# The output projection of a decoder layer as seven products of half matrices for eight, with the merge before it by pairs of column tiles and the mixer's first products in another order

## The chip, the core and the metric

One core of a Trainium2 chip runs the whole layer in one launch. Its engines are TensorE (PE in the rows; PEld is its loading of weights), VectorE (DVE), ScalarE (ACT), GpSimd (POOL) and SyncE (SP), which here only issues transfers. Each engine takes its instructions strictly in order and waits on semaphores for the others. The metric is device time in microseconds (us).

## The reference

```python
def reference(x, norm_mix, w_in, ...):
    ...
    gate_a, gate_b = jnp.split(jax.nn.sigmoid(g_merge), 2, axis=-1)
    merged = gate_a * (o_a @ w_up_nsa[layer]) + gate_b * (o_b @ w_up_gla[layer])
    x = x + merged @ w_out[layer]
    h = rmsnorm(x, norm_ffn[layer])
    x = x + (jax.nn.silu(h @ w_ffn_gate[layer]) * (h @ w_ffn_up[layer])) @ w_ffn_down[layer]
    return rmsnorm(x, norm_final)
```

`x` is 1024 tokens by 1024 channels, float32. Ahead of this stand two token mixers, `o_a` (sparse attention) and `o_b` (gated linear attention). `w_out` is 1024 by 1024, the SwiGLU's hidden width is 2816.

## The kernel before

All activations lie transposed: 128 channels on the partitions, tokens along the row. A tile of output is 128 channels by 512 tokens; `m` counts the eight tiles of channels (`NM`), `hf` the two halves of the tokens, `MH` is 4. A product of two float32 matrices is taken as three products of rounded parts: each operand is split into a high part (ACT copies it into the rounded type) and a low part (the operand less its high part, on POOL for weights, on DVE for activations), and PE does high x high, high x low and low x high. So each 128-channel block of the sum costs three matmuls of 128x512.

The stages that matter here, in the program's order:

- **Merge** (`merge_job`, L1324). For `m` = 0 to 7 and both halves PE multiplies the mixers' outputs with `w_up`; ACT takes the sigmoid of the gates `zz`, DVE and POOL gate and add. `let_merged` (L1317) then splits the result into the high and low part of a tile `mg`, 16 tiles in all. The product with `o_b` was computed earlier for the five `m` of `UP`; the other three do it here, with twice the PE work.
- **Output projection** (`out_job`, L1373). For each half, then each `m`, PE sums the eight blocks `mg` times `w_out` in one bank: 24 matmuls. DVE adds the bank to the tile `xn` of `x` (L1379), ACT squares it (L1383) and stores it to DRAM, DVE adds the squares up in `sacc` (L1388). The weights come through three rotating pairs of buffers: ACT makes `wh` (L368), POOL makes `wl` (L369).
- **Root.** When a half is complete, `two_parts` splits `sacc` into `sqh` and `sql`, `total` (L1409) lets PE sum them over the partitions with two matmuls (L1412), and `rms_root` (L447) makes `rbc` with two ACT and four DVE instructions. In the projection's second half DVE, ACT and DVE make the normalised first half (`first_block`, L1422): scale (L1426), high part, low part (L1429). `pairs[0].early` (L1460) splits the first four weights of the mixer ahead of time.
- **Channel mixer.** `Pair` holds one pair of weight tiles of the gate or of the up projection. The first three pairs use eight products of half matrices (`EIGHT`), the other nineteen seven (`SEVEN`). A half-matrix product (`Pair.product`, L1476) has 12 matmuls. `todo` is the list of products, in the program's order.

PE's order is the order in which the program is written, and so is DVE's through the mixer's first 26 products. ACT, POOL and SP are ordered by the scheduler of the framework, except where `keep_in_program_order` pins an instruction.

Of the kernel before, what the change touches and what calls it, by code (L numbers as in the profile page):

```python
# [10 lines left out]
F32 = mybir.dt.float32  # L11
# [91 lines left out]
SCRATCH = 2048  # L103
FINE, NGATE, AHEAD = 3, 2, 1200

UP = (1, 2, 4, 5, 7)


class Plan:
# [130 lines left out]
def layer_kernel(ctx, tc, a, outT):  # L240
# [1083 lines left out]
    def merge_job(m):  # L1324
        def make(getw):
            out, ps = [], {}
            for hf in range(2):
                def keep_ps(p, hf=hf):
                    ps[hf] = p

                def evac(p, hf=hf):
                    zz, u = fetched.pop((m, hf))
                    za, zb = zz[:, 0, :], zz[:, 1, :]
                    fetch()
                    tc.keep_in_program_order(S.activation(zz, zz, AF.Sigmoid))
                    let_merged(m - (hf == 0))
# [22 lines left out]
    mcst.release()  # L1359

# [3 lines left out]
    sacc = [None, None]  # L1364
    XN = {}

    last = []

    def let_last():
        while last:  # L1370
            last.pop(0)()

    def out_job(hf, m):  # L1373
        def make(getw):
            def evac(p):
                xv = XN[hf, m] = mid("xn")
                sq = mid("sacc")
                SP.dma_start(xv, a["xT"][:, m, hs(hf)])
                V.tensor_add(xv, p, xv)  # L1379

                def squares():

                    tc.keep_in_program_order(S.activation(sq, xv, AF.Square))  # L1383
                    S.dma_start(x1d[hf][m], xv)
                    if m == 0:
                        sacc[hf] = sq
                    else:
                        V.tensor_add(sacc[hf], sacc[hf], sq)  # L1388

                last.append(squares)  # L1390
                if m == NM - 1:
                    let_last()
            out = products(getw, ps_m, [t[:, 0, :] for t in mg[hf]], [t[:, 1, :] for t in mg[hf]], 0, evac)
            out[5:5] = [(0.0, let_last)]
            return out
        return a["w_out"][m], make
# [5 lines left out]
    def two_parts(t):  # L1402

        h, l = mid("sqh", F32R), mid("sql", F32R)
        tc.keep_in_program_order(S.activation(h, t, AF.Copy))
        tc.keep_in_program_order(P.tensor_tensor(l, t, f(h), OP.subtract))
        return h, l

    def total(st, parts, r):  # L1409

        for i, t in enumerate(parts):
            PE.matmul(st, onesr, t, start=i == 0, stop=i == 1)  # L1412
        rms_root(st, 512, float(D), r, [mid("nv"), mid("nq")])

    XB = {}

# [170 lines left out]
    fill.add(placed(dense([out_job(0, m) for m in range(NM)], False),  # L1587
                    [(15 + 6 * n, 0.0, lambda fn=fn: load(None, None, fn)) for n, fn in enumerate(first_loads())] + [(37 + 11 * n, 0.0, lambda nm=nm: pairs[0].early(nm)) for n, nm in enumerate(("11", "12", "21", "22"))]))
    fill.flush()
    work = dense([out_job(1, m) for m in range(NM)], False)  # L1590
    half_sums = {}
    fill.add(placed(work, [(11, 0.0, lambda: half_sums.update({0: two_parts(sacc[0])})),
                           (15, 450.0, lambda: total(ps_o(), half_sums[0], rbc[:, hs(0)]))]
                    + [(26 + 6 * m, 0.0, lambda m=m: first_block(m)) for m in range(NM)]))
    fill.flush()
    rows.release()


# [27 lines left out]


    MAKE = [[] for _ in range(26)]
    for n in range(NM):

        MAKE[1 + 3 * n // 4] += [(lambda n: normed(1, n), n)] + [(second_block, n - 1)] * (n > 0)
    MAKE[7].append((second_block, NM - 1))
# [17 lines left out]
    for i, (q, s) in enumerate(todo):  # L1650
        if i == 0:

            order.enter_context(tc.manual_schedule(engines={mybir.EngineType.DVE}))
        if i == 26:
            order.close()
        q.product(*s)
        if not q.kept and ahead:
            prepare(ahead.popleft())
        if i == 0:
            half_sums[1] = two_parts(sacc[1])  # L1660
        if i == 1:
            total(ps_o(), half_sums[1], rbc[:, hs(1)])
# [279 lines left out]
```

## Time and profile before

| | |
|---|---|
| median of three runs | 1577.27 us (1574.28, 1577.27, 1579.19) |
| the profiled execution | 1573.65 us |
| its span, first to last instruction | 1571.8 us |
| PE busy | 1556.8 us (99%) |
| DVE, ACT, POOL busy | 1014.1, 810.0, 719.7 us |

The page gives shares of the whole span; the stages have different limits. The merge ends and the projection begins at 831.5 us, the mixer's first matmul starts at 919.1 us. How to read the rows: `out<-in` are the program's names, `x` after them is how many instructions a row stands for, and in brackets stands the idle time before an instruction and what ended it.

### The profile page before, as it was taken

How to read it: one execution, taken by the hardware profiler on the slowest of the kernel's cores; microseconds unless marked ns; L12 is line 12 of the kernel's file. 1: busy time of each engine (PE TensorE's matmuls, PEld its weight loads, DVE VectorE, ACT ScalarE, POOL GpSimd, SP SyncE). 2: the span in 40 equal slices, each digit the busy share in tenths (PEclk: the TensorE clock that was granted, in tenths of full speed). 3: DMA queues.
4: the chain of work that ended last, by engine and by line, in shares of the span. 5: the costliest groups of instructions: out<-in, count | busy, mean ns of one | idle time of the engine just before them, and what ended most of it. 6: DMA issues, size and time to landing. Idle time of an engine off the chain costs nothing.

```text
span 1571.8 us, 23022 instructions
## 1 busy us (share of the span) xinstructions
PE 1556.8 (99%) x8031; PEld 1310.1 (83%) x8031; DVE 1014.1 (65%) x1630; ACT 810.0 (52%) x1615; POOL 719.7 (46%) x635
## 2 busy tenths in 40 slices
PE   9999999999999999999999999999999999999998
PEld 7888988888888888888888888888888888888887
DVE  7780487686777687667574577644444444499785
ACT  6241555575676686677654454334433334454542
POOL 6110466563223353253256520666666666555570
PEclk9999999999999999999999999999999999999999
DMA  5431112232111221131656622323222222795422
GB/s 180 140 104 62 61 55 79 97 107 81 45 51 57 71 83 56 51 109 60 205 184 211 215 83 81 114 101 106 102 101 101 101 101 101 282 340 161 141 88 107
DMA packets 109656, 179.86 MB, mean 114 GB/s; under 512 B 13394, under 2 KB 30435, under 8 KB 109540
## 3 DMA queue, kind: packets, MB, share of 16 engines
q1 hardware_dynamic: 105508, 171.96, 32.5%
q10 hardware_dynamic: 4032, 6.44, 1.1%
q8 instruction: 63, 1.03, 0.3%
q14 instruction: 53, 0.43, 0.1%
HBM read 128.27 MB, written 45.88 MB: 111 GB/s over the span
## 4 chain that ended last, share of the span: by engine, by line
PE 93%; DVE 4%; ACT 1%; issue 1%; DMA 1%; POOL 0%; SPq 0%; DVEq 0%; ACTq 0%; POOLq 0%
PE m L427 19%; PE d L427 10%; PE m L1484 9%; PE m L1485 9%; PE m L1483 9%; PE m L1873 4%; PE m L1871 4%; PE m L1872 4%; PE o L1210 4%; PE t L1201 3%; PE s L1122 2%; PE s L1123 2%; PE t L745 2%; PE t L747 1%; PE t L746 1%; PE t L880 1%
## 5 line engine op out<-in xcount | busy, mean ns | idle before, releaser
L369 POOL TENSOR_TENSOR wl<-wf,wh 128x512 fp32r<-128x512 f32 x106 | 146.3, 1385 | 275.6 <-ACT wh L368 274.8
L1484 PE MATMUL m<-xt,wh 128*128 128x512 f32 x412 | 160.3, 389 | 0.0
L1483 PE MATMUL m<-xt,wh 128*128 128x512 f32 x412 | 160.3, 389 | 0.0
L1485 PE MATMUL m<-xt,wl 128*128 128x512 f32 x412 | 160.3, 389 | 0.0
L1400 POOL TENSOR_TENSOR wl<-ws,wh 128x512 fp32r<-128x512 f32 x76 | 107.5, 1419 | 73.6 <-ACT wh L1399 73.6
L1400 POOL TENSOR_TENSOR wl<-wr,wh 128x512 fp32r<-128x512 f32 x69 | 92.0, 1333 | 70.0 <-ACT wh L1399 70.0
L1179 DVE TENSOR_TENSOR ptl<-t,pth 128x512 fp32r<-128x512 f32 (+1 forms) x168 | 99.5, 596 | 34.4 <-ACT pth L1178 31.4
L1399 ACT ACTIVATE wh<-wr 128x512 fp32r<-128x512 f32 x87 | 55.0, 632 | 121.0 <-POOL wl L1400 90.4
L1399 ACT ACTIVATE wh<-ws 128x512 fp32r<-128x512 f32 x76 | 48.0, 632 | 131.7 <-PE m L1484 112.6
L1178 ACT ACTIVATE pth<-t 128x512 fp32r<-128x512 f32 (+1 forms) x168 | 87.8, 524 | 53.2 <-PE t L1201 45.5
L1871 PE MATMUL m<-xb,wh 128*128 128x512 f32 x280 | 109.1, 389 | 0.3 <-DVE g L1545 0.3
L1400 POOL TENSOR_TENSOR wl<-wd,wh 128x512 fp32r<-128x512 f32 x56 | 82.1, 1468 | 58.9 <-ACT wh L1399 58.7
L1872 PE MATMUL m<-xb,wh 128*128 128x512 f32 x280 | 109.0, 389 | 0.0
L1873 PE MATMUL m<-xb,wl 128*128 128x512 f32 x280 | 108.9, 389 | 0.0
L1400 DVE TENSOR_TENSOR xb<-ar,xb 128x512 fp32r<-128x512 f32 x73 | 82.5, 1150 | 28.8 <-ACT xb L1399 28.8
L368 ACT ACTIVATE wh<-wf 128x512 fp32r<-128x512 f32 x106 | 66.2, 627 | 67.5 <-PE m L427 19.7
L427 PE MATMUL m<-hh,wh 128*128 128x512 f32 x240 | 99.9, 416 | 0.0
L427 PE MATMUL m<-hh,wl 128*128 128x512 f32 x240 | 93.8, 391 | 0.0
L427 PE MATMUL m<-hl,wh 128*128 128x512 f32 x240 | 93.6, 390 | 0.0
L1483 PEld LDWEIGHTS m<-xt,wh 128*128 128x128 f32 x412 | 77.4, 188 | 16.2
L1484 PEld LDWEIGHTS m<-xt,wh 128*128 128x128 f32 x412 | 77.4, 188 | 16.0
L1485 PEld LDWEIGHTS m<-xt,wl 128*128 128x128 f32 x412 | 77.4, 188 | 16.0
(422 smaller groups left out, 4569.4 us busy)
## 6 DMA issues: line engine op xcount, KB each, us to landing
ar<-actd SPq DMA_DIRECT2D x77, 256.0 KB, 3.0
wf<-in_w_t SPq DMA_DIRECT2D x58, 256.0 KB, 2.7
wr<-in_w_gate SPq DMA_DIRECT2D x44, 256.0 KB, 2.7
wr<-in_w_upf SPq DMA_DIRECT2D x44, 256.0 KB, 2.6
wd<-in_w_down SPq DMA_DIRECT2D x33, 256.0 KB, 5.1
zd<-zt SPq DMA_DIRECT2D x32, 256.0 KB, 2.0
zz<-zd SPq DMA_DIRECT2D x16, 512.0 KB, 4.6
wf<-in_w_out SPq DMA_DIRECT2D x32, 256.0 KB, 3.3
```

Source lines behind the costliest of these rows:

```text
L369: P.tensor_tensor(tl, wf, f(th), OP.subtract)
L427: PE.matmul(st["p"], w, x, start=k + i == 0, stop=k == n - 1 and i == 2)
L1178: S.activation(th[:, :c], pt[:, :c], AF.Copy)
L1179: V.tensor_tensor(tl[:, :c], pt[:, :c], f(th[:, :c]), OP.subtract)
L1399: S.activation(th, src, AF.Copy)
L1400: eng.tensor_tensor(tl, src, f(th), OP.subtract)
L1483: PE.matmul(ps, wh[:, c], xh, start=first and k == 0, stop=False, skip_group_check=not first)
L1484: PE.matmul(ps, wh[:, c], xl, start=False, stop=False, skip_group_check=not first)
L1485: PE.matmul(ps, wl[:, c], xh, start=False, stop=k == MH - 1, skip_group_check=not first)
L1871: PE.matmul(dst, wh[:, c], xh, start=first and p == 0, stop=False, skip_group_check=not first)
L1872: PE.matmul(dst, wh[:, c], xl, start=False, stop=False, skip_group_check=not first)
L1873: PE.matmul(dst, wl[:, c], xh, start=False, stop=p == NP - 1, skip_group_check=not first)
```

## The change

The 1024x1024 product is cut into halves in all three directions (channels in, channels out, tokens). Before, that is eight products of half matrices; now it is seven, after Winograd's form. They need sums of half matrices: of the weights S1 to S4 (`s1_out` to `s4_out`) and of the activations T1 to T4 (`t1_out` to `t4_out`). `OUT7` lists the products with the bank each adds to, and the order. One of its entries takes four steps, one for each tile `mp` of output channels, so there are 28 steps of 12 matmuls each. A bank is kept over several products, and after each step DVE adds it to an `xn` tile (`add_out`, L1691), so there are 28 such adds for 16 before.

The merge now goes by pairs of column tiles (`MO`: 0, 4, 1, 5, 2, 6, 3, 7), and `UP` holds 6 for 5. `let_merged` makes, of the second half's tiles 0 to 3, no `mg` but the difference to the first half (`xy`, T1), and POOL takes it from the tile `m + 4` (T2).

While a step runs, an order written out by hand (`todo_out`, `front_out`) places the work of DVE, POOL and ACT on the stretch: those three engines are now under `manual_schedule`. Weights are split by `prep_out`, three steps ahead (wh on ACT, wl on POOL). The squares' sums of the second half go to POOL, but two. The mixer's first eight products use the activations of block 11 first, in both pairs (`todo`); `high_part` and `low_part` make these from the end of the projection on, and `NEXT` places the second half's root after the mixer's first products.

```diff
-UP = (1, 2, 4, 5, 7)
+UP = (1, 2, 4, 6, 7)
...
+    MO = [m for j in range(MH) for m in (j, j + MH)]
+    halves = deque((m, hf) for m in MO for hf in range(2))
...
+    def let_merged():
+        if not merged:
+            return
+        za, hf, m = merged.pop()
+        j = m % MH
+        if hf and m < MH:
+            t = XY[j] = row("xy", shape=(2, 512))
+            V.tensor_sub(t[:, 0, :], za, firsts.pop(j))
+            return
+        t = mg[hf][m] = row("mg", F32R, (2, 512))
+        tc.keep_in_program_order(S.activation(t[:, 0, :], za, AF.Copy))
+        V.tensor_tensor(t[:, 1, :], za, f(t[:, 0, :]), OP.subtract)
+        if m < MH:
+            firsts[j] = za
+        elif hf:
+            x, y = XY[j][:, 0, :], XY[j][:, 1, :]
+            P.tensor_tensor(y, za, x, OP.subtract)
...
-    fill.add(dense([merge_job(m) for m in range(NM)], ready=early))
+    fill.add(dense([merge_job(m) for m in MO], ready=early))
...
+    first_out = [half_weights(a["w_out"][m], 0) for m in range(3)]
...
-    todo = [(q, s) for n in (0, 4) for q in pairs[:2] for s in EIGHT[n:n + 4]]
+    todo = [(q, EIGHT[n]) for ns in ((0, 2), (1, 3)) for q in pairs[:2] for n in ns]
+    todo += [(q, s) for q in pairs[:2] for s in EIGHT[4:]]
...
+    def s3_out(mp):
+        t = OW["S3", mp] = OW["11", mp]
+        V.tensor_sub(t, t, OW["21", mp])
+
+    def s2_out(mp):
+        t = OW["S2", mp] = OW["x", mp][:, 1, :]
+        P.tensor_tensor(t, OW["22", mp], OW["S3", mp], OP.subtract)
...
+    OUT7 = [("11", "11", "A", True, (0, 0)), ("12", "21", "B", True, (0, 0)), ("S2", "T2", "A", False, (1, 0)),
+            ("S3", "T3", "A", False, (1, MH)), ("22", "T4", "A", False, (0, MH)), ("S1", "T1", "B", True, (1, MH)),
+            ("S4", "22", "B", False, (1, 0))]
+    steps = [(p, mp) for p in OUT7 for mp in range(MH)]
...
+    def t3_out(j):
+        t = tmp["T3", j] = mid("to")
+        V.tensor_sub(t, XY[j][:, 1, :], f(mg[0][j][:, 0, :]))
+        V.tensor_sub(t, t, f(mg[0][j][:, 1, :]))
...
+    def place_out(nm, j):
+        parts_of(tmp.pop((nm, j)), OX[nm, j])
...
+    def pinned(src, th, tl, eng):
+        tc.keep_in_program_order(S.activation(th, src, AF.Copy))
+        tc.keep_in_program_order(eng.tensor_tensor(tl, src, f(th), OP.subtract))
+
+    def prep_out(i):
+        (nm, *_), mp = steps[i]
+        wh = wpool.tile([128, 512], F32R, name="wh", bufs=3)
+        wl = wpool.tile([128, 512], F32R, name="wl", bufs=3)
+        pinned(OW[nm, mp], wh, wl, P)
...
+    def add_out(i):
+        (_, _, bank, _, to), mp = steps[i]
+        xv = XN[to[0], to[1] + mp]
+        V.tensor_add(xv, PSB[bank, mp], xv)
...
+        at_out(5 + mp, t3_out, mp)
+        at_out(6 + mp, place_out, "T3", mp)
+        at_out(9 + mp, t4_out, mp)
+        at_out(10 + mp, place_out, "T4", mp)
+        at_out(14 + mp, t1_out, mp)
...
+        at_out(14 + mp, s1_out, mp)
+        at_out(14 + mp, s4_out, mp)
+        at_out(14 + mp, square_of, 0, mp)
+        at_out(15 + mp, square_sum, 0, mp)
...
+    front_out = {20: [lambda: square_of(0, NM - 1), lambda: square_sum(0, NM - 1), lambda: two_parts(0)]}
+    at_out(21, total, 0)
+    at_out(22, total_root, 0)
...
+    with tc.manual_schedule(engines={mybir.EngineType.DVE, mybir.EngineType.Pool, mybir.EngineType.Activation}):
+        for i in range(len(steps)):
+            product_out(i)
+            if i:
+                add_out(i - 1)
+            for fn in front_out.get(i, ()):
+                fn()
+            if i + 3 < len(steps):
+                prep_out(i + 3)
+            for fn in todo_out[i]:
+                fn()
...
-            q.prep(s, V if 3 <= i < 26 else P)
+            q.prep(s, V if 14 <= i < 26 else P)
...
+    NEXT = {0: [lambda: low_part(0, 5), lambda: high_part(0, 6), lambda: square_sum(1, MH - 1)],
+            1: [lambda: two_parts(1), lambda: low_part(0, 6), lambda: high_part(0, 7)],
+            2: [lambda: low_part(0, 7), lambda: total(1)], 3: [lambda: total_root(1)]}
```

What this does to the order of instructions, at three places. First DVE at the start of the projection's stretch in the kernel before. `minus` and `minusr` are two constants for the last stage, `xn<-m,xn` is the add of a bank to `x`, `sacc` the sum of squares:

```order
L1778 CAST minusr<-minus 128x128
L1379 TENSOR_TENSOR xn<-m,xn 128x512 x2
L1388 TENSOR_TENSOR sacc<-sacc 128x512
L1379 TENSOR_TENSOR xn<-m,xn 128x512
L1388 TENSOR_TENSOR sacc<-sacc 128x512
```

One add and one sum of squares stand there for each 24 matmuls of PE. Now DVE in the changed kernel, at steps 6 to 8 (L1645, L1646: the two subtractions that make a T3 in `to`; L1667: the low part of a T3, written over `mg`; L1691: the add):

```order
L1691 TENSOR_TENSOR xn<-m,xn 128x512
L1667 TENSOR_TENSOR mg<-to,mg 128x512
L1645 TENSOR_TENSOR to<-xy,mg 128x512
L1646 TENSOR_TENSOR to<-to,mg 128x512
L1691 TENSOR_TENSOR xn<-m,xn 128x512
```

Between two adds, that is per step of 12 matmuls, three instructions now stand on DVE that read two tiles of SBUF each. Next the end of the first half on DVE in the changed kernel (steps 18 to 22; `sql` is the low part of the sum of squares, `nv` and `rbc` the root):

```order
L1691 TENSOR_TENSOR xn<-m,xn 128x512
L1396 TENSOR_TENSOR sacc<-sacc 128x512 x2
L1691 TENSOR_TENSOR xn<-m,xn 128x512
L1396 TENSOR_TENSOR sacc<-sacc 128x512
L1404 TENSOR_TENSOR sql<-sacc,sqh 128x512
L1691 TENSOR_TENSOR xn<-m,xn 128x512 x2
L451 TENSOR_SCALAR nv<-o 128x512
```

The low part `sql` comes after all the sums, and it was POOL's before (L1406). Last PE around the two matmuls that add up the first half's squares, before and then now:

```order
L427 MATMUL m<-mg,wl 128x512
L1412 MATMUL o<-sqh,onesr 128x512
L1412 MATMUL o<-sql,onesr 128x512
L427 MATMUL m<-mg,wh 128x512 x2
L427 MATMUL m<-mg,wl 128x512
```

```order
L1684 MATMUL m<-xb,wh 128x512
L1685 MATMUL m<-xb,wh 128x512
L1686 MATMUL m<-xb,wl 128x512
L1410 MATMUL o<-sqh,onesr 128x512
L1410 MATMUL o<-sql,onesr 128x512
L1684 MATMUL m<-xb,wh 128x512
```

Before, they stood in the third product of the second half, with 13 products still to come before the mixer. Now they stand behind step 21 of 0 to 27, six steps before the mixer. PE has 48 matmuls fewer in all (7832 for 7880).

## Rows read from the trace of the kernel before

**Rows 1.** Page, part 1 (busy us) and part 4 (the chain's engines).
```profile
PE 1556.8 (99%) x8031; PEld 1310.1 (83%) x8031; DVE 1014.1 (65%) x1630; ACT 810.0 (52%) x1615; POOL 719.7 (46%) x635
...
PE 93%; DVE 4%; ACT 1%; issue 1%; DMA 1%; POOL 0%; SPq 0%; DVEq 0%; ACTq 0%; POOLq 0%
```

**Rows 2.** Stretches: us, then busy us of PE PEld DVE ACT POOL, clock.
```profile
781.00:831.50 50.50, 50.50 (x224) 41.84 (x223) 39.11 (x47) 27.49 (x38) 28.15 (x20) 1.00 0.52 167
831.50:918.80 87.30, 87.30 (x386) 72.27 (x385) 51.00 (x57) 38.16 (x65) 49.32 (x36) 1.00 0.65 211
918.80:982.00 63.20, 63.20 (x280) 52.27 (x280) 48.18 (x72) 30.77 (x50) 4.72 (x3) 1.00 0.19 67
```

**Rows 3.** Timeline of PE: first matmuls of the projection, first of the mixer.
```profile
831.51 0.62 PE L427 MATMUL m<-mg,wh 128*128 128x512 f32 x2
...
919.08 0.39 PE L1483 MATMUL m<-xb,w 128*128 128x512 f32 x1
```

**Rows 4.** Groups of PE by line and shape: count, busy us, mean ns.
```profile
L427 PE MATMUL m<-mg,wh 128*128 128x512 f32 x256 | 78.9, 389 | 0.0
...
L427 PE MATMUL m<-mg,wl 128*128 128x512 f32 x128 | 49.8, 389 | 0.0
```

**Rows 5.** Waits of PE from 600 to 1300 us: total, times, longest.
```profile
PE t L1201 <- DVE ptl L1179: 1.0, 2, 0.7
```

**Rows 6.** Groups of DVE, 831.5 to 945 us.
```profile
L1388 DVE TENSOR_TENSOR sacc<-sacc 128x512 f32<-128x512 f32 x14 | 15.8, 1127 | 11.7 <-ACT sacc L1383 11.5
L1379 DVE TENSOR_TENSOR xn<-m,xn 128x512 f32<-128x512 f32 x16 | 11.0, 686 | 20.2 <-DMA xn<-in_xT 19.5 <-PE m L427 0.7
...
L1419 DVE SCALAR_TENSOR_TENSOR xn<-xn,gains,rbc 128x512 f32<-128x512 f32 x8 | 5.9, 748 | 0.0
...
L1429 DVE TENSOR_TENSOR xb<-xn,xb 128x512 fp32r<-128x512 f32 x8 | 5.5, 688 | 1.7 <-ACT xb L1428 1.4
```

**Rows 7.** Timeline of DVE: start us, us, instruction.
```profile
838.14 1.21 DVE L1778 CAST minusr<-minus 128x128 fp32r<-128x128 f32 x1
...
885.48 1.67 DVE L454 TENSOR_TENSOR nv<-nv,nq 128x512 f32<-128x512 f32 x1
...
888.94 0.68 DVE L1379 TENSOR_TENSOR xn<-m,xn 128x512 f32<-128x512 f32 x1
889.54 0.73 DVE L1426 SCALAR_TENSOR_TENSOR xn<-xn,gains,rbc 128x512 f32<-128x512 f32 x1
...
892.01 1.36 DVE L1388 TENSOR_TENSOR sacc<-sacc 128x512 f32<-128x512 f32 x1 [0.35 <-ACT sacc L1383]
```

**Rows 8.** Timeline of POOL, the same stretch and the merge's end.
```profile
835.03 4.25 POOL L369 TENSOR_TENSOR wl<-wf,wh 128x512 fp32r<-128x512 f32 x3 [3.29 <-ACT wh L368]
...
885.19 1.41 POOL L369 TENSOR_TENSOR wl<-wf,wh 128x512 fp32r<-128x512 f32 x1 [2.70 <-ACT wh L368]
...
891.54 2.99 POOL L369 TENSOR_TENSOR wl<-wf,wh 128x512 fp32r<-128x512 f32 x2 [3.07 <-ACT wh L368]
```

**Rows 9.** Groups of POOL and of ACT, 831.5 to 945 us.
```profile
L369 POOL TENSOR_TENSOR wl<-wf,wh 128x512 fp32r<-128x512 f32 x30 | 42.9, 1442 | 35.0 <-ACT wh L368 34.9
L1464 POOL TENSOR_TENSOR w<-wr,w 128x512 fp32r<-128x512 f32 x4 | 5.2, 1292 | 0.0
...
L368 ACT ACTIVATE wh<-wf 128x512 fp32r<-128x512 f32 x30 | 18.7, 625 | 25.3 <-DVE xn L1379 11.7 <-PE m L427 6.6 <-DMA wf<-in_w_out 3.2
L1383 ACT ACTIVATE sacc<-xn 128x512 f32<-128x512 f32 x16 | 9.9, 620 | 4.8 <-DVE xn L1379 4.8
...
L450 ACT ACTIVATE nq<-o,eps 128x512 f32<-128x512 f32 x2 | 1.4, 688 | 5.3 <-PE o L1412 3.2 <-DVE xn L1379 2.1
```

**Rows 10.** Page, part 6: issues, KB each, us to landing.
```profile
wf<-in_w_out SPq DMA_DIRECT2D x32, 256.0 KB, 3.3
```

More of the change, by code (lines that the diff above doesn't have):

```diff
@@ L1365, in layer_kernel @@
     XN = {}
[L1367 to L1396, printed above, removed]
     def split(src, th, tl, eng):
@@ L1400, in split, with square_of, square_sum, two_parts @@
         eng.tensor_tensor(tl, src, f(th), OP.subtract)
[L1402 to L1411, printed above, removed]
+    def square_of(hf, m):
+        t = SQ[hf, m] = mid("sacc")
+        S.activation(t, XN[hf, m], AF.Square)
+        S.dma_start(x1d[hf][m], XN[hf, m])
+    def square_sum(hf, m):
+        t = SQ.pop((hf, m))
+        if sacc[hf] is None:
+            sacc[hf] = t
+        else:
+            (P if hf and m not in (MH - 2, MH - 1) else V).tensor_tensor(sacc[hf], sacc[hf], t, OP.add)
+    SQ, half_sums, root_tmp = {}, {}, {}
+    def two_parts(hf):
+        h, l = half_sums[hf] = mid("sqh", F32R), mid("sql", F32R)
+        S.activation(h, sacc[hf], AF.Copy)
+        V.tensor_tensor(l, sacc[hf], f(h), OP.subtract)
+    def total(hf):
+        st = root_tmp[hf] = ps_o()
+        for i, t in enumerate(half_sums[hf]):
             PE.matmul(st, onesr, t, start=i == 0, stop=i == 1)
-        rms_root(st, 512, float(D), r, [mid("nv"), mid("nq")])
+    def total_root(hf):
+        rms_root(root_tmp[hf], 512, float(D), rbc[:, hs(hf)], [mid("nv"), mid("nq")])
     XB = {}
@@ L1585, in placed @@
         return work
[L1587 to L1594, printed above, removed]
@@ L1595, in layer_kernel, with load_out @@
-    fill.flush()
+    OW, PSB = {}, {}
+    def load_out(nm, mp):
+        if nm == "21":
+            OW["x", mp] = fa.tile([128, 2, 512], F32, name="wx", tag="xT3", bufs=MH)
+            t = OW["x", mp][:, 0, :]
+        else:
+            tag, bufs = ("ws", 4) if nm == "11" or ("S3", mp) in OW else ("w7", 6)
+            t = fa.tile([128, 512], F32, name="wo", tag=tag, bufs=bufs)
+        OW[nm, mp] = t
+        m, o = mp + MH * (nm[0] == "2"), MH * (nm[1] == "2")
+        load(t, a["w_out"][m][:, o:o + MH, :].rearrange("p a b -> p (a b)"))
@@ new lines, in layer_kernel, with parts_of, t2_out @@
+    steps = [(p, mp) for p in OUT7 for mp in range(MH)]
+    OX, tmp = {}, {}
+    for j in range(MH):
+        OX["11", j] = OX["T3", j] = mg[0][j]
+        OX["21", j] = OX["T4", j] = mg[0][MH + j]
+        OX["22", j] = mg[1][MH + j]
+    def parts_of(t, x):
+        pinned(t, x[:, 0, :], x[:, 1, :], V)
+    def t2_out(j):
+        OX["T2", j] = fa.tile([128, 2, 512], F32R, name="xb", tag="xb", bufs=8)
+        parts_of(XY[j][:, 1, :], OX["T2", j])
+    def t3_out(j):
+        t = tmp["T3", j] = mid("to")
+        V.tensor_sub(t, XY[j][:, 1, :], f(mg[0][j][:, 0, :]))
+        V.tensor_sub(t, t, f(mg[0][j][:, 1, :]))
@@ new lines, in t4_out, with t1_out, load_xn @@
+    def t4_out(j):
+        t = tmp["T4", j] = mid("to")
+        V.tensor_sub(t, f(mg[0][MH + j][:, 0, :]), XY[j][:, 1, :])
+        V.tensor_add(t, t, f(mg[0][MH + j][:, 1, :]))
+    def place_out(nm, j):
+        parts_of(tmp.pop((nm, j)), OX[nm, j])
+    def t1_out(j):
+        OX["T1", j] = fa.tile([128, 2, 512], F32R, name="xb", tag="xb", bufs=8)
+        parts_of(XY[j][:, 0, :], OX["T1", j])
+    def load_xn(hf, m):
+        XN[hf, m] = mid("xn")
+        load(XN[hf, m], a["xT"][:, m, hs(hf)])
@@ new lines, in pinned, with product_out @@
+    def pinned(src, th, tl, eng):
[6 more added lines that the diff above has]
+        pinned(OW[nm, mp], wh, wl, P)
+        OW["parts", i] = wh, wl
+    def product_out(i):
+        (nm, x, bank, first, to), mp = steps[i]
+        wh, wl = OW.pop(("parts", i))
+        if first:
+            PSB[bank, mp] = ps_m()
+        ps = PSB[bank, mp]
+        for k in range(MH):
+            xh, xl, c = OX[x, k][:, 0, :], OX[x, k][:, 1, :], bs(k)
+            PE.matmul(ps, wh[:, c], xh, start=first and k == 0, stop=False, skip_group_check=not first)
+            PE.matmul(ps, wh[:, c], xl, start=False, stop=False, skip_group_check=not first)
+            PE.matmul(ps, wl[:, c], xh, start=False, stop=k == MH - 1, skip_group_check=not first)
@@ new lines, in add_out, with at_out @@
+    def add_out(i):
+        (_, _, bank, _, to), mp = steps[i]
+        xv = XN[to[0], to[1] + mp]
+        V.tensor_add(xv, PSB[bank, mp], xv)
+    todo_out = [[] for _ in range(len(steps))]
+    def at_out(i, fn, *args):
+        todo_out[i].append(lambda: fn(*args))
+    wload = first_loads()
+    for mp in range(MH):
+        at_out(mp, t2_out, mp)
+        if mp < 2:
+            at_out(mp, load_out, "12", 2 + mp)
+        at_out(2 + mp, s3_out, mp)
+        at_out(3 + mp, s2_out, mp)
+        at_out(5 + mp, t3_out, mp)
[3 more added lines that the diff above has]
+        at_out(14 + mp, t1_out, mp)
+        at_out(4 + mp, load_xn, 1, mp)
+        at_out(8 + mp, load_xn, 1, MH + mp)
+        at_out(12 + mp, load_xn, 0, MH + mp)
+        at_out(11 + mp, load_out, "12", mp)
+        at_out(14 + mp, s1_out, mp)
+        at_out(14 + mp, s4_out, mp)
+        at_out(14 + mp, square_of, 0, mp)
+        at_out(15 + mp, square_sum, 0, mp)
+        if mp < MH - 1:
+            at_out(17 + mp, square_of, 0, MH + mp)
+            at_out(min(18 + mp, 19), square_sum, 0, MH + mp)
+        at_out(18 + mp, pairs[0].early, ("11", "12", "21", "22")[mp])
@@ new lines, in layer_kernel @@
+    front_out = {20: [lambda: square_of(0, NM - 1), lambda: square_sum(0, NM - 1), lambda: two_parts(0)]}
+    at_out(21, total, 0)
+    at_out(22, total_root, 0)
+    for i in range(20, len(steps) - 1):
+        (_, _, _, _, to), mp = steps[i]
+        at_out(i + 1, square_of, 1, to[1] + mp)
+        at_out(min(i + 2, len(steps) - 1), square_sum, 1, to[1] + mp)
+    for m, i in enumerate((24, 24, 25, 25, 26, 27)):
+        at_out(i, high_part, 0, m)
+        if m < 5:
+            todo_out[i + 1].insert(0, lambda m=m: low_part(0, m))
@@ new lines, in layer_kernel @@
+    for n, fn in enumerate(wload):
+        at_out(7 + n, load, None, None, fn)
+    for mp in range(MH):
+        load_out("11", mp)
+    for mp in range(2):
+        load_out("12", mp)
+    for mp in range(MH):
+        load_xn(0, mp)
+    for nm in ("21", "22"):
+        for mp in range(MH):
+            load_out(nm, mp)
+    for i, (wh, wl) in enumerate(first_out):
+        OW["parts", i] = [t.rearrange("p a b -> p (a b)") for t in (wh, wl)]
+    with tc.manual_schedule(engines={mybir.EngineType.DVE, mybir.EngineType.Pool, mybir.EngineType.Activation}):
[9 more added lines that the diff above has]
+                fn()
+        add_out(i)
+        square_of(1, MH - 1)
@@ L1628, in layer_kernel @@
     MAKE = [[] for _ in range(26)]
[L1629 to L1632 removed]
+    for m, i in enumerate((4, 4, 5, 5, 6, 6, 7, 7)):
+        MAKE[i].append((lambda m: high_part(1, m), m))
+        MAKE[i + 1].insert(0, (lambda m: low_part(1, m), m))
     for j in range(MH):
@@ L1658, in layer_kernel @@
             prepare(ahead.popleft())
[L1659 to L1662, printed above, removed]
+        for fn in NEXT.get(i, ()):
+            fn()
         if i < len(todo) - 1:
```

41 lines of the change are left out of this document (21 added, 20 removed).

## The prediction, made before the changed kernel had run

> **What bounds the kernel now.** I read the page's shares first: PE is busy 1556.8 of the 1571.8 us span and makes 93% of the chain, DVE 4% [rows 1]. So a removed matmul is worth its time wherever PE has no wait. The windows by stage come next: in the projection (831.5 to 918.8 us) PE is busy 87.30 of 87.30 us at a granted clock of 1.00, DVE 51.00, ACT 38.16, POOL 49.32 [rows 2]. The waits of PE say the same: from 600 to 1300 us the longest is 0.7 us [rows 5]. The first matmul of the projection starts at 831.51 and the first of the mixer at 919.08 [rows 3], with 384 matmuls of the projection [rows 4] and two of the root between them: 87.57 / 386 = 0.227 us each. The mean of one matmul in its group, 389 ns, is longer because matmuls are pipelined; the distance is what counts. A step of 12 takes 2.72 us.
>
> **What goes.** 28 steps of 12 are 336 matmuls for 384: 48 x 0.227 = 10.9 us of PE, and all of it counts, since PE has no wait to lose there. Behind the projection PE's work is the same.
>
> **What costs nothing.** In the merge, four low parts of DVE become four differences of the same shape, ACT loses four copies, and POOL gets four differences more: at 1.3 to 1.5 us each some 6 us, beside POOL's 28.15 busy of 50.5 [rows 2]; if that cover were gone, the last one alone would show. The merge's pairs of tiles need no more of PE, and one more product with `o_b` is made earlier, one fewer here. The loads are 23 for 32, and landing takes 3.3 us [rows 10]; the latest wanted one starts when a merge tile is free (about 834) and is used by DVE about 848. POOL's split of the third weights, begun at 835.03 before and 4.25 us for three [rows 8], comes early enough: the first two steps' weights are split in the merge, and the third are wanted at 831.5 + 2 x 2.72 + 0.45 = 837.4; I count about 1 us of cover, and 1 to 2 us of wait without it. ACT was busy 38.16 of 87.3 and does some 30 copies more at 0.62 [rows 9], beside its waits. POOL is busy 4.72 of 63.2 us at the mixer's start [rows 2], so the splits that `prep` now leaves to it have room.
>
> **What DVE has to do instead.** Before, DVE had one add and one sum for 5.4 us of PE. Now there are an add and three instructions with two operands in SBUF for 2.72 us, in steps 6 to 13. Such an instruction takes 0.69 us alone (L1429: 688 ns) [rows 6], an add from the bank 0.60 in a row (888.94 to 889.54) [rows 7]: 0.60 + 3 x 0.69 = 2.67 of 2.72 us. There is hardly anything left, and POOL is beside it.
>
> What POOL does to DVE stands in rows. At 892.01 a sum of squares takes 1.36 us where others take 0.69 [rows 7], and POOL has begun a pair of weights at 891.54 [rows 8]. At 885.48 an instruction of the root takes 1.67, beside POOL's at 885.19 [rows 7, 8]. The group of the sums has a mean of 1127 ns [rows 6]: (1127 - 690) / 670 = 0.65 of them met POOL. The add from the bank does not suffer: mean 686, with POOL beside it or not [rows 6]. So a meeting costs DVE 0.67 us, at most 0.98, for each POOL instruction.
>
> DVE is free for the new work at 838.14 + 1.21, about 839.4 [rows 7]. PE wants `sql` behind step 21, at 831.5 + 22 x 2.72 = 891.3. What DVE has in order up to `sql`:
> - 20 adds from the bank x 0.60 = 12.0
> - 48 with two operands in SBUF (8 low parts of T2 and T1, 8 of S3 and S4, 12 for T3, 12 for T4, 7 sums, `sql`) x 0.69 = 33.1
> - two hops over ACT that nothing hides at the end (the last square 0.62, the copy to `sqh` 0.63) [rows 9] = 1.25
> - meetings: POOL has 28 instructions in that time (weights' low parts, S2, S1, the first early weights). On this case's own share 0.65 of 48 instructions is more than POOL has, so nearly every POOL instruction meets one; I take 24 of 28 x 0.67 = 16.1.
>
> Sum 62.4, so `sql` is there at 901.8 and PE has lost 10.5 us by then. It need not lose it all at `sql`: DVE's lag shows earlier, at the first steps that read the last T3 (step 12), T4 (16) and T1 (20). It is the same lag and is counted once.
>
> The bounds of this term: with no meetings DVE's own work would be done at 885.8, and the chain behind step 19's end at 885.9 (add, square, sum, copy, `sql`: 3.3) gives 889.2, before PE comes: no wait. With 28 x 0.98 it is 913.1, a wait of 21.8. I take 24 because 0.65 of the sums met POOL and POOL now stands beside a DVE that hardly pauses. PE's wait is nothing as long as no more than (891.3 - 885.8) / 0.67, about 8 of 28, meet.
>
> The Trainium skill, "SBUF — State Buffer", section "SBUF: two separate sides", says of the port pair that VectorE and GpSimd share that it is held for a whole instruction and the other engine fully blocks meanwhile. By that a meeting could cost DVE the 1.29 us that POOL takes alone. The rows disagree on the size: 1.36 or 1.67 in place of 0.69, and POOL's pair takes 2.99 us with a DVE instruction in it, 1.49 each. I go by the rows; the rule is the last rival below.
>
> **The second half's root.** `total(1)` stands behind the mixer's third product. From 901.8, PE has the root's matmuls 0.45, six steps 16.3 and three products 8.2: 926.8. DVE has 8 adds x 0.60 = 4.8, 8 scalings x 0.748 = 6.0 [rows 6], 11 x 0.69 = 7.6 and one more 0.69: 19.1. ACT's logarithm for the first root (688 ns [rows 9]) is behind a weight copy that waits for step 22, so DVE idles 3.3. Of 15 POOL instructions I let 9 meet, 6.0. Two ACT hops, 1.25. Sum 29.7: `sql` is there at 931.5, a wait of 4.7. Bounds: no meetings 23.7 us, no wait; 15 x 0.98 gives 38.4 us and a wait of 13.4.
>
> **Sum.** -10.9 + 10.5 + 4.7 = +4.3 us. The profiled execution took 1573.65 (span 1571.8, 1.85 around it), so that one would be 1578.0; the median of the runs, 1577.27, is 3.6 above the profiled execution, which makes 1581.6. The corners on the median are -10.9 (1566.4) and -10.9 + 21.8 + 13.4 = +24.3 (1601.6).
>
> **Rivals.**
> *DVE keeps pace: faster.* PE waits nowhere as long as no more than 8 of POOL's 28 instructions meet one of DVE's. For it: POOL's and DVE's low parts both start from an ACT copy, and ACT makes one at a time, so they can fall beside each other's gaps; the eight low parts of L1429 cost 688 ns, as if alone, though POOL was busy 49.32 of 87.30 [rows 2, 6]. Against: the sums met POOL in 0.65 of cases. Then 1577.3 - 10.9 = 1566.4, 0.7% faster. Chance 0.30.
> *Somewhat more than half meet: no change.* 16 of 28 and 6 of 15: the first wait is 8 x 0.67 = 5.4 less, 5.1; the second 3 x 0.67 = 2.0 less, 2.7. Net -3.1, 1574.2. It is the forecast's mechanism with a smaller count: the sums' own share, 0.65, lies between the two [rows 6]. Chance 0.19.
> *POOL shuts DVE out for its whole instruction: much slower.* 28 x 1.29 + 33.1 + 1.3 = 70.5, with the adds beside it, gives 909.9, a wait of 18.6; then 15 x 1.29 + 14.3 + 4.5 = 38.2 for PE's 25.0, 13.2. Net +20.9, about 1598. The rows of POOL's pairs speak against it [rows 8]. That is the skill's rule named above. Chance 0.06.
> *The change does not do what it says:* excluded, 48 matmuls are gone from PE's order. *The clock:* it is 1.00 in all three stretches [rows 2], and no row shows PE after a wait of several us [rows 5]; the range's top has room for some of it, and other things that make it slower have 0.03.
>
> **How the numbers follow.** What a measurement of this kernel can tell from no change is 0.3%, 4.7 us. The forecast has 0.42: 1581.6, its own range 1576 to 1590; since 1577.3 + 4.7 = 1582.0 runs through it, 0.25 is slower and 0.17 the same. The first rival is faster, 0.28, with 0.02 the same (waits of a few us). The second is the same, 0.14, with 0.05 faster. The last rival and the rest are slower, 0.09. Together faster 0.33, same 0.33, slower 0.34. The range goes from the first rival's 1566 to 1594, which leaves out the last rival and the forecast's high corner.
>
> **What would show it.** Right: PE waits for DVE's `sql` behind step 21 or, before it, for the low parts of T3, T4, T1 behind steps 11, 15 and 19; those waits sum to about 10 us, a second one stands in the mixer's third product, and DVE's two-SBUF instructions have means near 0.9 to 1.0 us in the projection. The stretch from the projection's first matmul to the mixer's first is then 338 x 0.227 = 76.7 us and the waits. Wrong: means near 0.7 us, or PE without waits above 1 us there; then the first rival has it. Also wrong: a first wait on weights in steps 2 to 5, which I cost at nothing, or an early PE wait on POOL.

## The result and the profile after

The changed kernel takes 1588.64 us (median of six runs, 1587.21 to 1589.63) against 1576.15 for the kernel before (six runs, 1574.28 to 1579.19). The ratio is 1.0077, 95% interval 1.0063 to 1.0090: slower by 0.8%, 12.5 us between the medians. The profiled execution took 1588.36, its span 1586.6, 14.8 us more than the span before [rows 1]. The experiments' times are medians of fast runs; one run of 2187.63 us, at a granted clock of 0.66, is left out of the 1570.01 us below.

The page of the changed kernel, parts 1 and 4:

```profile
PE 1554.2 (98%) x7983; PEld 1303.0 (82%) x7983; DVE 1063.7 (67%) x1673; ACT 814.7 (51%) x1623; POOL 754.7 (48%) x652
...
PE 86%; DVE 7%; issue 2%; ACT 2%; POOL 1%; DMA 1%; SPq 0%; DVEq 0%; POOLq 0%; ACTq 0%
```

The chain now runs over DVE for 7% where it was 4% [rows 1]. PE's busy time fell by only 2.6 us although 48 matmuls went; matmuls at half clock, below, are part of the reason. The windows by stage of the changed kernel, columns as in [rows 2]:

```profile
781.00:831.50 50.50, 50.50 (x224) 41.84 (x223) 40.33 (x47) 25.82 (x35) 33.80 (x22) 1.00 0.60 203
831.50:860.00 28.50, 28.21 (x125) 23.05 (x124) 26.77 (x26) 10.73 (x17) 23.51 (x16) 1.00 0.62 203
860.00:885.00 25.00, 20.64 (x81) 15.92 (x80) 24.32 (x29) 9.32 (x17) 9.69 (x7) 0.93 0.47 159
885.00:905.00 20.00, 16.17 (x66) 11.62 (x64) 19.68 (x19) 8.58 (x16) 18.26 (x12) 1.00 0.21 80
905.00:925.00 20.00, 16.56 (x61) 13.21 (x62) 12.77 (x17) 10.61 (x19) 12.87 (x10) 0.83 0.32 118
925.00:945.00 20.00, 15.90 (x68) 12.30 (x67) 18.25 (x20) 9.23 (x16) 11.51 (x8) 1.00 0.11 41
```

The merge is as it was. Then DVE is busy 24.32 of 25 and 19.68 of 20 us: full. PE, which had no gap before [rows 2], is busy about four fifths of the time from 860 us on, and twice its granted clock is below 1. PE's waits from 832 to 965 us (in total, times, longest):

```profile
PE o L1410 <- ACT sqh L1403: 6.8, 2, 5.6
PE m L1684 <- ACT mg L1666: 4.4, 3, 3.1
PE m L1489 <- DVE xb L1434: 2.7, 1, 2.7
PE m L1489 <- DVE xt L1434: 1.2, 1, 1.2
PE m L1686 <- POOL wl L1667: 0.9, 2, 0.6
```

With four smaller ones they sum to 17.2 us, for nothing above 0.7 before [rows 5]. The first two name ACT, but ACT's copy had itself just been waiting for DVE, as its timeline ahead of step 12 shows:

```profile
868.31 0.63 ACT L1666 ACTIVATE mg<-to 128x512 fp32r<-128x512 f32 x1 [2.65 <-DVE to L1646]
```

DVE's groups in the stretch that the prediction summed up (839.3 to 909.1 us):

```profile
L1691 DVE TENSOR_TENSOR xn<-m,xn 128x512 f32<-128x512 f32 x21 | 14.3, 680 | 0.0
L1667 DVE TENSOR_TENSOR xb<-xy,xb 128x512 fp32r<-128x512 f32 x8 | 11.7, 1463 | 0.1
L1396 DVE TENSOR_TENSOR sacc<-sacc 128x512 f32<-128x512 f32 x7 | 8.6, 1222 | 0.9 <-ACT sacc L1388 0.7
L1667 DVE TENSOR_TENSOR mg<-to,mg 128x512 fp32r<-128x512 f32 x8 | 7.8, 974 | 0.5
L1645 DVE TENSOR_TENSOR to<-xy,mg 128x512 f32<-128x512 f32 x4 | 6.5, 1626 | 0.0
```

The adds from a bank are as short as before (680 for 686 [rows 6]); of the 48 instructions with two operands in SBUF 29 take 1.16 us or more for 0.69, and the mean of the 48 is 1.20. A piece of DVE's timeline at steps 6 and 7, and POOL's instructions beside it:

```profile
858.15 1.77 DVE L1645 TENSOR_TENSOR to<-xy,mg 128x512 f32<-128x512 f32 x1
859.96 0.69 DVE L1646 TENSOR_TENSOR to<-to,mg 128x512 f32<-128x512 f32 x1
860.57 0.69 DVE L1691 TENSOR_TENSOR xn<-m,xn 128x512 f32<-128x512 f32 x1
861.35 0.69 DVE L1667 TENSOR_TENSOR mg<-to,mg 128x512 fp32r<-128x512 f32 x1
861.96 1.79 DVE L1645 TENSOR_TENSOR to<-xy,mg 128x512 f32<-128x512 f32 x1
```

```profile
857.64 1.74 POOL L1667 TENSOR_TENSOR wl<-wx,wh 128x512 fp32r<-128x512 f32 x1
861.92 1.29 POOL L1667 TENSOR_TENSOR wl<-wx,wh 128x512 fp32r<-128x512 f32 x1 [2.54 <-ACT wh L1666]
```

One POOL instruction per step, one DVE instruction of 1.77 or 1.79 per step, and a step costs DVE 3.81 us (858.15 to 861.96) where PE needs 2.72. The ends tell how they meet. POOL's instruction of 861.92 ends at 863.21 and DVE's of 861.96 at 863.75, 0.54 us later; for the pair before it (857.64 and 858.15) the difference is 0.54 us too. All 29 long instructions of DVE up to `sql` end 0.54 to 0.55 us after one of POOL's 30 has ended, wherever they began. The other way round, a POOL instruction that begins while DVE's runs takes about 1.74 us for 1.29 (at 857.64). So the two do not share: one waits until the other is done.

PE's timeline at step 12, at the first half's sum and at the mixer's start:

```profile
869.03 0.47 PE L1684 MATMUL m<-mg,wh 128*128 128x512 f32 x1 [3.14 <-ACT mg L1666]
...
869.58 0.63 PE L1686 MATMUL m<-mg,wl 128*128 128x512 f32 x1
870.00 0.63 PE L1684 MATMUL m<-mg,wh 128*128 128x512 f32 x1
...
908.44 0.79 PE L1410 MATMUL o<-sqh,onesr 128*128 128x512 f32 x1 [5.65 <-ACT sqh L1403]
...
928.05 0.39 PE L1488 MATMUL m<-xb,w 128*128 128x512 f32 x1
```

After the waits of 3.14 and 5.65 us the matmuls stand 0.43 us apart (869.58 to 870.00) and not 0.227. In both places the granted clock is 0.50, which is 1.2 GHz for 2.4:

```profile
869.60:872.90 3.30, 3.30 (x9) 2.63 (x8) 3.30 (x4) 1.15 (x2) 3.19 (x2) 0.50 0.70 234
909.20:913.90 4.70, 4.70 (x12) 3.73 (x12) 1.11 (x2) 1.78 (x4) 4.70 (x4) 0.50 0.31 112
```

Eight matmuls at the first place and eleven at the second, 0.20 us longer each and a little more around the sum, lose 1.6 and 2.3 us, 3.9 in all.

The account: the projection's first matmul stood at 832.47, so from there to the mixer's first at 928.05 it is 95.6 us, against 87.57 [rows 3] and against 76.7 without a wait. The loss there is 18.9, and about 6 more in the mixer's first products. Against 10.9 saved that makes 14, and 15 with the 0.96 us by which the projection starts later (832.47 for 831.51); the span grew by 14.8.

### The profile page after: what moved, and what is told of

The parts are those of the page before. It is cut to its first block, busy times and chain, and to the rows that moved or that the text cites. A ratio compares the mean times of both kernels' runs of the same rounds, so it can differ in the third digit from the quotient of the medians.

```text
span 1586.6 us, 22969 instructions
## 1 busy us (share of the span) xinstructions
PE 1554.2 (98%) x7983; PEld 1303.0 (82%) x7983; DVE 1063.7 (67%) x1673; ACT 814.7 (51%) x1623; POOL 754.7 (48%) x652
## 4 chain that ended last, share of the span: by engine, by line
PE 86%; DVE 7%; issue 2%; ACT 2%; POOL 1%; DMA 1%; SPq 0%; DVEq 0%; POOLq 0%; ACTq 0%
PE m L427 14%; PE d L427 10%; PE m L1489 8%; PE m L1490 8%; PE m L1488 8%; PE m L2035 4%; PE m L2033 4%; PE m L2034 4%; PE o L1210 3%; PE t L1201 3%; PE s L1122 2%; PE s L1123 2%; PE t L745 2%; PE t L746 1%; PE t L747 1%
## 5 line engine op out<-in xcount | busy, mean ns | idle before, releaser
L369 POOL TENSOR_TENSOR wl<-wf,wh 128x512 fp32r<-128x512 f32 x77 | 105.9, 1379 | 242.0 <-ACT wh L368 240.6
L1384 POOL TENSOR_TENSOR wl<-wr,wh 128x512 fp32r<-128x512 f32 x75 | 102.1, 1362 | 85.6 <-ACT wh L1383 84.6
L427 PE MATMUL d<-hh,wh 128*128 128x512 f32 x224 | 89.4, 399 | 0.0
```

Of the source, the lines that this page charges most:

```text
L369: P.tensor_tensor(tl, wf, f(th), OP.subtract)
```

## The experiments

All are read against the kernel before on the same chip (medians 1576.7, 1576.9 and 1577.0 us), and against 1588.6 of the changed kernel.

**Without POOL's low parts (steps 9 to 27).**

```
-        pinned(OW[nm, mp], wh, wl, P)
+        if i < 9:
+            pinned(OW[nm, mp], wh, wl, P)
+        else:
+            S.activation(wh, OW[nm, mp], AF.Copy)
+            S.activation(wl, OW[nm, mp], AF.Copy)
```

> The changed kernel, but the weights of steps 9 to 27 get no low part from POOL: ACT copies the source a second time in its place. This leaves the weights' low parts out of the result; PE's instructions and DVE's are the same. Theory 1 (POOL's instructions lengthen DVE's two-SBUF ones, and DVE's lag is what PE waits for): in the changed kernel 29 of 48 such instructions up to sql are longer by 24.4 us in all, 0.84 each; without the 14 POOL instructions of steps 9 to 22 the lag at sql falls by 14 x 0.84 = 11.8 us, PE's waits in the projection from about 15 to 3 us, the clock's fall with them, and the time to about 1570 (1565 to 1577). Rival 2 (the number of DVE's instructions and their order alone make DVE late): DVE's order is unchanged, so within 3 us of 1588.6. Rival 3 (the hand-written places of total(0) and the roots are too early whatever DVE does): PE still waits over 4 us at the first half's sql, 1585 or more.

1577.14 us, ratio 1.0001 (0.9991 to 1.0011): 11.5 us back with not one instruction of PE or DVE changed. The span of DVE from its first new instruction to the end of `sql` is 57.6 us (842.91 to 900.55) for 69.7: 12.1 less, where theory 1 said 11.8. Its groups there:

```profile
L1396 DVE TENSOR_TENSOR sacc<-sacc 128x512 f32<-128x512 f32 x7 | 6.9, 987 | 0.9 <-ACT sacc L1388 0.7
L1667 DVE TENSOR_TENSOR mg<-to,mg 128x512 fp32r<-128x512 f32 x8 | 6.2, 780 | 0.5
...
L1645 DVE TENSOR_TENSOR to<-xy,mg 128x512 f32<-128x512 f32 x4 | 3.2, 806 | 0.0
```

L1645 fell from 1626 to 806 ns. Rival 2 (within 3 us of 1588.6) is out. The time I expected, 1570, was not reached: PE still waits 4.4 us for `sqh` (3.3 at the first half's sum, 1.1 at the second's), and 2.5 and 0.9 at the mixer's start, nearly as before. POOL still had 15 instructions up to `sql` (S1, S2, the first low parts, the mixer's weights), each of which lengthened one of DVE's, by 11.6 us in all; and the mixer's waits were not touched.

**The same low parts on DVE.** Here `late` collects the subtraction, and DVE does it a step later, behind the add:

```
+            S.activation(wh, OW[nm, mp], AF.Copy)
+            late.append(lambda: V.tensor_tensor(wl, OW[nm, mp], f(wh), OP.subtract))
```

> The changed kernel, the low parts of the weights of steps 9 to 27 made by DVE instead of POOL, one step after their high part. Theory 1 (a POOL instruction costs DVE about as much as doing it would): per instruction +0.69 on DVE and -0.84 of meetings, over 14 of them up to sql -2 us, so 1583 to 1590, and DVE's two-SBUF mean falls from 1.2 to about 0.9 us. Rival 2 (DVE's count alone): 14 x 0.69 = +9.7 us at the first root and +3.4 at the second, about 1602.

1586.91 us (ratio 1.0054, 1.0038 to 1.0071), as theory 1 expected, 15 us under rival 2. DVE does 14 instructions more up to `sql` and needs 64.5 us for it (842.69 to 907.20), 5.2 less than with POOL's help; the mean of its instructions with two operands in SBUF is 0.89 us. PE gains little from that, since it now waits for the low parts themselves:

```profile
PE m L1691 <- DVE wl L1678: 5.0, 5, 1.6
PE m L1489 <- DVE xb L1434: 2.1, 2, 1.5
PE o L1410 <- ACT sqh L1403: 1.5, 1, 1.5
```

**POOL as busy, with one operand.** In place of each low part POOL copies the source twice (`P.tensor_copy(wl, OW[nm, mp])`, ACT still makes `wh`).

> The changed kernel, but in place of each low part of the weights of steps 9 to 27 POOL copies the source twice into the same tile (one operand; 0.61 us each in the kernel before, so about as long busy). The low parts are left out of the result. It asks what in a POOL instruction lengthens DVE's. If POOL's reading and writing SBUF is enough: DVE's two-SBUF instructions are as long as in the changed kernel, 1586 to 1590. If it takes POOL's two operands: as in the run without these POOL instructions, 1575 to 1579.

1585.68 us (ratio 1.0054, 1.0033 to 1.0076). The time is nearly that of the first case, but it doesn't decide: here PE also waits 3.2 us for POOL's own copies. DVE's rows do. A piece of its timeline, and POOL's beside it:

```profile
861.32 1.00 DVE L1667 TENSOR_TENSOR mg<-to,mg 128x512 fp32r<-128x512 f32 x1
862.24 1.09 DVE L1645 TENSOR_TENSOR to<-xy,mg 128x512 f32<-128x512 f32 x1
863.36 0.98 DVE L1646 TENSOR_TENSOR to<-to,mg 128x512 f32<-128x512 f32 x1
```

```profile
861.71 3.78 POOL L1678 CAST wl<-wo 128x512 fp32r<-128x512 f32 x4
```

Each DVE instruction is 0.3 to 0.4 us longer, not 1.1, and POOL's copies are lengthened to about 0.95 each. DVE's way to `sql` is 63.8 us (840.07 to 903.88), halfway between 57.6 and 69.7. So POOL's one operand is enough to lengthen DVE. The long instructions again end 0.54 to 0.55 us after one of POOL's; 36 of them lose 18.5 us up to `sql`, 0.51 each, since most of POOL's are copies of 0.61 us and sooner done.

**Fewer instructions on DVE.** The second subtraction of each T3 and T4 is left out (L1646, L1652).

```
-        V.tensor_sub(t, t, f(mg[0][j][:, 1, :]))
...
-        V.tensor_add(t, t, f(mg[0][MH + j][:, 1, :]))
```

> The changed kernel without the second subtraction of each T3 and T4 (the low part of a first-half block is left out of them): DVE has 8 two-SBUF instructions fewer up to sql, 6.5 us in the trace of the changed kernel. POOL's work is the same. Theory 1 (DVE is over its capacity, each instruction taken from it brings sql forward): PE's waits up to sql fall from 15.1 by about 6 us and the clock's loss by 1 to 2: 1580 to 1584. Rival (PE waits for single places, the first T3 above all, not for the sum of the work): the wait at step 12 goes and the one at sql grows, 1587 or more.

1583.16 us (1.0041, 1.0026 to 1.0057), inside theory 1's 1580 to 1584. But the rival's first half was right too: the waits at steps 12 to 16 went, and the one for `sqh` stayed at 5.7, since `sql` moved up only as far as PE did.

**DVE nearly alone.** Beside that, POOL's low parts, S1 and S2 and the mixer's first weights are left out (second ACT copies, or nothing).

> As the run without the second subtractions, and POOL does nothing in the projection but sums of squares of the second half: the low parts of all weights, and of the mixer's first four, are a second ACT copy, S2 is an ACT copy and S1 isn't formed (all these values are left out of the result). PE's instructions are those of the changed kernel. Theory 1: DVE has 20 x 0.60 + 40 x 0.69 + 1.25 = 40.9 us for 51.9 of PE, so no wait over 1 us up to sql; some 2 to 4 us stay at the mixer's start; the clock stays at full: 1567 to 1571, the saving of 48 matmuls nearly in full. Rival (the places of total and of the roots, or the mixer's new order, cost by themselves): waits over 6 us stay, 1574 or more.

1574.43 us, ratio 0.9984 (0.9975 to 0.9993). Windows and groups from DVE's first new instruction to `sql`:

```profile
837.90:893.20 55.30, 54.66 (x240) 44.68 (x239) 37.78 (x61) 39.04 (x72) 0.00 (x0) 1.00 0.54 185
```

```profile
L1664 DVE TENSOR_TENSOR mg<-to,mg 128x512 fp32r<-128x512 f32 x8 | 5.5, 692 | 9.1 <-ACT mg L1663 9.1
...
L1644 DVE TENSOR_TENSOR to<-xy,mg 128x512 f32<-128x512 f32 x4 | 2.7, 683 | 0.0
```

POOL is at 0.00, every DVE instruction back at 0.68 to 0.69, DVE has 17 us to spare and PE waits 0.8 us up to there in place of 11.8. That half of theory 1 stands. The expected 1567 to 1571 was missed, and the time is its rival's (1574 or more, though with waits of 5.8 us in all where it had over 6): PE waits 3.6, 0.7 and 0.7 us at the mixer's start, with ten matmuls at half clock (2.2 us) behind the first.

**The root's place.** DVE's timeline in the changed kernel shows where:

```profile
908.42 0.69 DVE L1404 TENSOR_TENSOR sql<-sacc,sqh 128x512 fp32r<-128x512 f32 x1 [0.69 <-ACT sqh L1403]
909.03 1.28 DVE L1691 TENSOR_TENSOR xn<-m,xn 128x512 f32<-128x512 f32 x2
915.71 0.69 DVE L451 TENSOR_SCALAR nv<-o 128x512 f32<-128x512 f32 x1 [5.40 <-ACT nq L450]
```

```profile
914.47 0.63 ACT L1666 ACTIVATE wh<-wo 128x512 fp32r<-128x512 f32 x1 [3.49 <-PE m L1685]
915.01 0.67 ACT L450 ACTIVATE nq<-o,eps 128x512 f32<-128x512 f32 x1
```

ACT's logarithm (L450) stands behind a weight copy that waits for PE. Two runs move the root ahead of the copy (in the first with all else as in the changed kernel, in the second with DVE nearly alone); a third is the second once more, for its trace:

```
-    at_out(22, total_root, 0)
+    front_out[22] = [lambda: total_root(0)]
```

> The changed kernel with the first half's root placed ahead of the weights' split in step 22, so that ACT's logarithm doesn't stand behind a weight copy that waits for step 22's end. Nothing is left out. Theory 1 with the root as a second chain: DVE idles 5.40 us before the root, 4 to 4.5 of it go, and the waits at the mixer's first products (2.7 and 1.2 us) and at the second root (1.2 us) go or shrink: 1583 to 1586. Rival: DVE has so much work behind the root that the mixer's waits stay, within 1.5 us of 1588.6.

> The run in which DVE is nearly alone (POOL's splits and sums of weights and the second subtractions left out as there), with the first half's root ahead of the split of the weights in step 22. It asks for what is left there: waits of 5.1 us at the mixer's first products, with 2.2 us of half clock behind them. Theory: ACT's logarithm stands behind a weight copy, DVE idles 4.4 us at the root, and now that DVE has time the root's 4 us reach the mixer: waits there under 2 us, the clock at full, 1567 to 1571. Rival (what follows the root on DVE, with POOL's sums of squares beside it, is the limit, as in the run with the root first and all of POOL's work): 1573 to 1576.

> The run with DVE nearly alone and the root first once more, for its trace (the same values are left out). At 1570.3 us, 4.1 less than without the root first, theory says that the root's logarithm starts about 4 us earlier behind the total, DVE's root follows within 2 us, and PE's waits at the mixer's first products are under 2 us in all where they were 5.0, with no matmul at half clock behind them.

In the changed kernel it brings nothing: 1589.64 us (1.0078, 1.0062 to 1.0094). DVE's idle time falls from 5.40 to 1.28 us, but the next scalings are longer (3.48 us for two, 1.40 before that), and PE's wait for `xb` only goes from 2.7 to 1.9, while the one at the second root grows from 1.2 to 1.9, with seven matmuls at half clock behind it. With DVE nearly alone it brings 4.4: 1570.01 us (0.9954, 0.9937 to 0.9971). PE's waits there, in the trace of the run after it (a single run of 1572.27 us):

```profile
PE o L1410 <- ACT sqh L1403: 1.8, 2, 1.2
PE m L1489 <- DVE xb L1434: 1.4, 1, 1.4
PE m L1489 <- DVE xt L1434: 0.9, 1, 0.9
```

No matmul there is at half clock. The waits at the mixer's blocks are 2.3 us, a little over the 2 expected. But the logarithm came only 1.0 us earlier behind the total and not 4 (4.5 us after it for 5.6; ACT has a queue of copies here that the kernel proper doesn't have). The `xb` blocks that PE waits for are ready 3.1 us earlier behind `sql`; the other 2 us are two DVE instructions that met POOL in the trace without the root first and did not meet it in this one. So what the root's place alone is worth stays open.

**The total two steps later.**

```
-    at_out(21, total, 0)
-    at_out(22, total_root, 0)
+    at_out(23, total, 0)
+    front_out[24] = [lambda: total_root(0)]
```

> The changed kernel with PE's total of the first half behind step 23 instead of 21, and its root ahead of the split of the weights in step 24. Nothing is left out. Theory 1 (DVE's work is what is late): the wait at sql, 5.8 us, shrinks to near nothing, and comes back at the mixer's first products, which wait for the root and what DVE makes from it: 1586 to 1591. Rival (the place of the total, two steps too early, costs the 5.8 us): 1582 to 1584.

1589.95 us (1.0088, 1.0071 to 1.0106). PE no longer waits at the total; it waits 3.7 (in two) and 0.9 us for `xb` in the mixer, and 2.9 for a weight's high part. The place of the total is not the loss.

**The other two parts of the change, alone.** The kernel before with the merge's order only:

> The kernel before with only the merge's new order (0, 4, 1, 5, 2, 6, 3, 7) and the other list of five tiles whose first product is made earlier; projection, mixer and all else as before. Theory: the merge keeps PE busy either way, 1576 +- 3. Rival: the merge order costs the 0.96 us by which the projection starts later in the changed kernel (832.47 for 831.51), or more.

1575.55 us, ratio 0.9995 (0.9986 to 1.0005): no cost. And the changed kernel with the mixer's first products in the old order (`todo` as before, `high_part` of block 5 at step 26, of 6 and 7 at step 27):

> The changed kernel with the mixer's first eight products in the order of the kernel before (block 21 is wanted by the second product, not by the fifth), all eight high parts made by the end of the projection. Nothing is left out. Theory 1: DVE, late as it is, has blocks 21 ready later than PE wants them, the mixer's waits grow by 3 to 8 us: 1591 to 1597. Rival (the new order is itself a cause of the loss): faster than 1587.

1594.63 us (1.0119, 1.0103 to 1.0135): the new order is worth 6 us in this kernel; it is no cause of the loss.

## Why the prediction was right, and where its sizes were off

The time lies inside the range, 1566 to 1594, but that says little: the range holds a faster kernel, an unchanged one and a slower one, and each had a chance of about a third. What the experiments bear out is the forecast's mechanism, DVE late because POOL lengthens its instructions.

- *10.9 us go:* right. With POOL's work and eight subtractions away and the root first, 7.0 of them show in the time (1577.0 to 1570.0), and waits of 4.6 us are left in the trace of that kernel.
- *The merge, the loads and ACT cost nothing:* right for the merge (its own run). No wait of PE in the stretch names a load. ACT had room, but its order delayed the first half's root (below). The third weights were in time.
- *DVE's sum up to `sql`:* the mechanism was right, the term for meetings too small. Predicted 62.4 us, measured 69.7. I let 24 of 28 POOL instructions meet DVE at 0.67 each, 16.1 us. In the trace POOL has 30 there, 29 DVE instructions are longer, by 24.4 us in all: 0.84 each, and the longest, 1.80, is 1.11 over. Their mean was foretold as 0.9 to 1.0 us and was 1.20. All else was 45.3 for 46.3 predicted. The share of 0.65 from the sums [rows 6] came from a DVE that paused between instructions; here DVE hardly pauses, and each of POOL's instructions but one held up one of DVE's.
- *The price of a meeting:* the prediction read 1.36 and 1.67 us in place of 0.69 as a price of 0.67, at most 0.98, and POOL's pair of 2.99 us as 1.49 each. The ends in the same rows [rows 7, 8] say more. DVE's instruction of 885.48 ends at 887.15, 0.55 us after POOL's, which ran from 885.19 for 1.41 us; the one of 892.01 had begun 0.47 us into POOL's. So a meeting costs what is left of POOL's instruction when DVE's begins, less 0.14 us (0.69 less 0.55; an estimate from these rows): up to 1.11, in the mean 0.84. The 0.67 was one case of this and no price.
- *The rule of the Trainium skill* ("SBUF — State Buffer", "SBUF: two separate sides") is that the loser is shut out for the whole instruction. The prediction held that the rows disagree with it; they agree, by the ends above. Its last rival, at 1.29 a meeting, was still too dear (36 us for 24.4), since DVE's instructions mostly began when POOL's was some way on, and the 0.14 comes off. That the contention is with any GpSimd instruction that reads SBUF, as the section has it, agrees with the copies of one operand (0.3 to 0.4 us each).
- *PE's waits up to `sql`:* predicted 10.5 us. The places were nearly right (the last T3 at step 12, short waits at 15, 16, 20 and 21, then `sql`). When PE starts on the first half's sum, at 908.44, it is 16.0 us late: 264 matmuls from 832.47 would have ended at 892.4. This is DVE's sum again, with `sql` done at 909.1 for 901.8. The waits that the profile lists come to 11.8 of it; matmuls at half clock at step 12 (1.6) and wider gaps around each wait lie in the rest. Behind the sum come 2.8 us more, 2.3 of them at half clock. Half clock had no price in the sum, only "room for some of it" at the range's top: the second term that failed, and the smaller one.
- *The second root:* predicted 4.7. Its own wait was 1.2, but blocks `xb` and `xt` took 2.7 and 1.2 ahead of and behind it: 5.1 in all. That the amount is near is luck, for the place was another: the first half's root, whose 5.40 us of DVE's idle I had at 3.3, was late already.
- *The first rival* (DVE keeps pace) is what the run with DVE nearly alone shows up to `sql`; in the changed kernel POOL met DVE 29 times of 30. *No change* failed with it.

The forecast was +4.3 us, the medians differ by 12.5. In the profiled execution 18.9 us were lost up to the mixer where 10.5 were forecast, and about 6 behind it for 4.7: the meetings, 24.4 us for 16.1, are the term that was too small, and the half clock, at nothing, the one that was left out.

## What to carry to other kernels

An engine that is the bound gives a saving back when its feeders fill up: add up each feeder's instructions per step against the new length of a step, and add for VectorE what GpSimd's instructions beside it cost, taking one meeting for every GpSimd instruction once VectorE has no pauses. To price a meeting, compare the two ends in a trace: an instruction that always ends the same time after the other engine's has waited for it, and its length only says how early it began. Work "hidden" on GpSimd is then not free; the run that moved it onto VectorE needed less of VectorE. And look behind a wait of TensorE for matmuls at half clock, and price them from the trace too.

## What the runs showed of the hardware

- A 128x512 float32 VectorE instruction with two SBUF operands takes 0.69 us alone. Where it met a GpSimd instruction it ended 0.54 to 0.55 us after that one's end, in all 29 cases of the changed kernel up to `sql`, and took up to 1.80 us. A GpSimd subtraction of 1.29 us that began while VectorE's ran took about 1.74. With one operand in PSUM VectorE's stays at 0.68.
- Beside GpSimd copies with one operand (0.61 us alone) VectorE's instruction took 0.98 to 1.09 us in the rows shown.
- After waits of 3.14 and 5.65 us TensorE ran eight and eleven matmuls 0.43 us apart, at a granted clock of 0.50, then 0.227 again. The length of the last wait alone does not tell: after one of 2.70 us in the changed kernel the matmuls stayed 0.23 us apart; in the run with the second subtractions left out eight came at 0.43 soon after one of 2.69, and in the run with the low parts on VectorE seven behind waits of 1.63 and 1.45 us.
